# Odd layer of a two-layer backbone: where raw weights land, the order of weight splits and norms, two cells moved between stages, and the first loads of attention

## The chip, the cores and the metric

The kernel runs on one core of one Trainium2 chip. The metric is the device time of one execution in microseconds (us). A core has TensorE (matmuls, PE in the profile; weight loads are PEld), VectorE (DVE), ScalarE (ACT), GpSimd (POOL) and SyncE (SP), each with an instruction queue of its own that is worked off in order. In this kernel SP, POOL and ACT also issue DMA transfers.

## The reference, cut to what matters

Two layers run over 2048 latent tokens and 256 context tokens (16 and 2 tiles of 128). Layer 0 is the even mixer; layer 1, which the change touches, is the odd mixer:

```python
def odd_mixer(h, hc, w_in, q_gain, k_gain, rpb, w_out, update_ctx):
    def heads(u):
        bsz, n, _ = u.shape
        q, k, v, z = jnp.split(u, 4, axis=-1)
        sh = lambda t: t.reshape(bsz, n, C_HEADS, C_HD)
        return rms_norm(sh(q), q_gain), rms_norm(sh(k), k_gain), sh(v), z

    q_x, k_x, v_x, z_x = heads(jnp.dot(h, w_in))
    q_c, k_c, v_c, z_c = heads(jnp.dot(hc, w_in))
    o = neighborhood_attention(q_x, k_x, v_x, k_c, v_c, rpb)
    y = jnp.dot(o.reshape(h.shape[0], h.shape[1], C_WIDTH) * jax.nn.silu(z_x), w_out)
```

`h` and `hc` are the normalised and modulated tokens (1024 wide), `w_in` is 1024 x 4096, there are 16 heads of 64, and the attention of a token sees a window of 8 rows by 16 columns of the token grid, with a bias and a column mask, and the context tokens.

## The kernel before

**Numbers in two parts.** A float32 operand is split into a high part (rounded to the engine's fp32r) and a low part (the rest). A product is three matmuls, high x high, high x low and low x high (`mm3_steps`, L129 to L131 in the profile), accumulated in one bank. A raw weight tile of 128 x 512 is copied by ScalarE to the high part (L106 `w0h<-wraw`) and subtracted by VectorE to the low part (L383 `w0l<-wraw,w0h`).

**Weights of layer 1.** `w_in` is cut into eight blocks j of 512 columns: 0 and 1 are q, 2 and 3 k, 4 and 5 v, 6 and 7 z. Four fit on chip at a time. `OD_PLACE` gives each block one of four places, which the tiles `w0` to `w3` name: blocks 2, 3, 0, 1 take places 0, 1, 2, 3, and later blocks 4, 5, 6, 7 take the same ones. `od_steps` loads a block in eight steps k of 128 rows, through `split_steps` (L366): a raw tile in the ring `wraw` of three buffers, a load on SP (L380), and the two halves of the split. It is a generator that yields after each second step. `pump` takes one such stride after every fourth step of the stage's matmuls, from the first generator in the list `ahead`.

**Cells.** A cell (t, j) is tile t of 128 tokens times block j: 24 matmuls into one bank. `stream` runs cells in a given order and prepares (`prep`, with the normalisation L328, transposes L331, and the two parts of the result L343 and L344) or reloads the next tile where one is done; when a block has had its last cell, `done(j)` appends the generator of the block that follows in its place (`nxt`).

**odd_qk** runs blocks 2, 3, 0, 1 over all tiles. After a q or k cell, ScalarE squares the bank, VectorE sums by head (L1238), GpSimd raises to the power -0.5 (`rpow`, L200 and L202), and VectorE multiplies the bank by it (L1241, `onat`). The cell then waits in `pend`, and `fin` is called for it at the sixth step of a later cell: four transposes on TensorE (L1249), copies by ScalarE and VectorE, and stores to scratch in HBM: Q1 and K1 by SP, K1t by GpSimd (L1286, four of 512 columns at once where four tiles have been collected). The last two tiles, 16 and 17, run block by block at the end: 0, 1, 2, 3 and then 6. Block 6 is half of the gate z: `gate` (tanh on ScalarE, L1301 on VectorE), transposed and stored to z1 by GpSimd (L1253).

**odd_vz** runs the rest, tiles from the last to the first. It begins with (17, 7), (16, 7), (17, 4), (16, 4), (17, 5), (16, 5). A v cell is copied by ScalarE and stored to V1 by GpSimd (`store_v`); a z cell is gated and transposed (L1341). Between them `weave` puts the steps of `maxes`, 0.57 of them for a step of a cell: it finds the largest score of each query and head (matmuls L1376 and L1383, VectorE L1389), with tiles `mk`, `mq`, `mtab`, the memsets of `mz` (L1350) and a mask added by GpSimd (L1361). The results go to M1.

**odd_attention** loads by SP, through `load` (L111): per pair of heads j the queries (`q`, with a row from M1), the context's keys `kc`, four chunks of keys `kt`, values `ov` from V1 and V1c, and the bias tables `tab`, two of 128 x 1034, to which GpSimd adds the column mask `maskk` (L1479). Scores (`st`, L1482 and L1483) of the context's keys need no table; those of the chunks get one added by VectorE (L1646) before ScalarE's exponential. VectorE sums the context's exponentials (L1505), GpSimd the others (L1521). The order of the first loads before is: q(0,1), kt chunk 0, V, tables, kc, q(0,0), kt chunk 1, V1c, maskk.

A program orders the instructions of each engine from a list schedule; `issue_after` puts what is issued within it behind a given instruction.

Of the kernel before, what the change touches and what calls it, by code (L numbers as in the profile page):

```python
# [17 lines left out]
P = 128  # L18
# [70 lines left out]
class Kern:  # L89
    def __init__(self, tc, nc, ins, scr):  # L90
        self.tc, self.nc, self.i, self.scr = tc, nc, ins, scr
        self.n = 0
        self.ahead, self.calls, self.chain = [], 0, None
# [64 lines left out]
    def pump(self):  # L158

        self.calls += 1  # L160
        while self.ahead and self.calls % 4 == 0:
            if next(self.ahead[0], self) is not self:
                break
            self.ahead.pop(0)
# [32 lines left out]
    def rpow(self, out, in_, mul, add):  # L197
# [4 lines left out]
        g.tensor_tensor(out=out, in0=out, in1=self.mhalf[:, : shp[1]], op=ALU.pow)  # L202
# [830 lines left out]
    def even_mix(self, e1, win, hT):  # L1033
# [3 lines left out]
        with ExitStack() as es:  # L1037
# [94 lines left out]

            def ahead():
                for j in (2, 3):
                    yield from self.od_steps(win, j, ws)
# [60 lines left out]
    def od_steps(self, dst, j, ws):  # L1196
        n = self.OD_PLACE[j]
        steps = self.split_steps(dst, j, ws[n // 2], self.i["w_od"][:, j], KD, 512, f"w{n}", 1)
        for k, _ in enumerate(steps):
            if k % 2:  # L1200
                yield

    def odd_qk(self, ws, win, hT):
# [7 lines left out]
        with ExitStack() as es:  # L1211
# [5 lines left out]
            self.ahead += [self.od_steps(win, 0, ws), self.od_steps(win, 1, ws)]  # L1217
            pend, kt = [], {}

            def cell(t, j):  # L1220
# [4 lines left out]
                                       (lambda k: wh[:, k, :], lambda k: wl[:, k, :]), range(KD))  # L1225
# [15 lines left out]
                nc.vector.tensor_tensor(out=n[:].rearrange("p (h d) -> p h d", h=8), in0=ps[:],  # L1241
                                        in1=ss[:].unsqueeze(2).to_broadcast([P, 8, 64]), op=ALU.mult)
                pend.append((t, j, n))

            def fin(t, j, n):
# [9 lines left out]
                self.act(hi[:], ps[:], AF.Copy, scale=qkg[:, z : z + 1])  # L1255
# [3 lines left out]
                if z == 0 or t < NCT:  # L1259
# [7 lines left out]
                    else:  # L1267
                        store_k((hi, lo), j0, t * P, P)
# [10 lines left out]
                if r0 == 6:  # L1279
                    store_k(kt.pop(j), j0, CTX + g * 512, 512)  # L1280

            def store_k(parts, j0, o, w):

                for u, x in enumerate(parts):
                    for i in range(2):
                        nc.gpsimd.dma_start(self.K1t[j0 : j0 + 4, i, u * 64 : u * 64 + 64, o : o + w].rearrange("j d t -> d j t"),  # L1286
                                            x[i * 64 : i * 64 + 64].bitcast(F32))

            nxt = {2: 4, 3: 5, 0: 6, 1: 7}
            done = lambda j: j in nxt and self.ahead.append(self.od_steps(win, nxt[j], ws))  # L1290
            cells = self.cells(list(range(NT)), (2, 3, 0, 1), lambda t, j: j > 1 or t >= NCT)[:-8]
            cells += [(t, j) for j in (0, 1, 2, 3, 6) for t in (NT - 2, NT - 1)]
            for _ in self.stream(cells, hT, cell, lambda t: self.prep(1, t, self.x1, pp, ("px", 2)), done):
                self.pump()
            while pend:
                fin(*pend.pop(0))

# [18 lines left out]
    def odd_vz(self, ws, win, hT):  # L1316
# [3 lines left out]
        with ExitStack() as es:  # L1320
# [6 lines left out]
            def cell(t, j):  # L1327
# [4 lines left out]
                                          (lambda k: wh[:, k, :], lambda k: wl[:, k, :]), range(KD))  # L1332
# [76 lines left out]
            cells = [(t, j) for j in (7, 4, 5) for t in (NT - 1, NT - 2)]  # L1409
# [5 lines left out]
    def odd_attention(self, out, right, left, wout):  # L1415
# [4 lines left out]
        with ExitStack() as es:  # L1420
# [56 lines left out]
            def mask(tabs):  # L1477
                for tb in tabs:
                    nc.gpsimd.tensor_tensor(out=tb[:], in0=tb[:], in1=mk[:], op=ALU.add)  # L1479
# [340 lines left out]
```

## Time and profile before

| | us |
|---|---|
| time, median of 3 runs (lowest to highest) | 3648.87 (3647.48 to 3651.03) |
| the profiled execution: its time | 3651.72 |
| its span on the core | 3649.9 |
| mean granted TensorE clock | 0.985 of full |
| odd_qk, from the first matmul on layer 1's weights | about 2150 to 2602 of the span |
| odd_vz | about 2602 to 3065 |
| odd_attention | about 3065 to 3475 |
| output projection | from about 3475 |

How to read the rows below: in the view of waits a row says which engine and line waited, for which instruction, how long in total, how many times, and the longest. In a row of slices stand the stretch, its length, the busy time of TensorE, weight loads, VectorE, ScalarE and GpSimd with their counts, the granted clock, and what the DMA engines did. A row of the timeline gives start and length in us, the engine, the line, the operation, out<-in, and the idle time ahead of it with what ended it. A row of the chain of waits gives start, length and what was waited for or worked on.

### The profile page before, as it was taken

To read this page: it belongs to the slowest core of one execution; us is meant where nothing else is said; L and a number is where in the kernel's file an instruction comes from. 1 tells how busy PE (TensorE), PEld (TensorE's weight loads), DVE (VectorE), ACT (ScalarE), POOL (GpSimd) and SP (SyncE) were. 2 spreads that over 40 slices of the span, in tenths; PEclk is the share of its full clock that TensorE was granted. 3 is DMA by queue.
4 is the path that set the end of the run, shared out by engine and by line. 5 is a ranking of instruction groups with operands and counts; after the bars stand their busy time and mean duration, and the time that the engine had idled before them with its cause. 6 is when DMAs were issued, how large, how long until landed. Compare 5 with 4: busy or idle time off the path is not lost.

```text
span 3649.9 us, 51809 instructions
## 1 busy us (share of the span) xinstructions
PE 3552.6 (97%) x18404; PEld 2750.0 (75%) x18404; DVE 2355.6 (65%) x4860; ACT 1433.1 (39%) x2741; POOL 1200.8 (33%) x1336
## 2 busy tenths in 40 slices
PE   8999999999999999999999999999899999999899
PEld 6988998888886666665657878888688887555577
DVE  4677666888876666688664435545578784666721
ACT  5545551111115555555553224444422223555510
POOL 1433330101011222112311234333344434777743
PEclk9999999999999999999999999999999999999999
DMA  7455472222242232334533544445743437778554
GB/s 255 146 154 157 135 207 82 86 76 89 74 131 66 76 102 72 93 92 116 164 98 116 186 160 126 146 142 170 226 145 123 140 119 204 209 206 220 176 179 149
DMA packets 364372, 512.19 MB, mean 140 GB/s; under 512 B 25825, under 2 KB 243889, under 8 KB 358210
## 3 DMA queue, kind: packets, MB, share of 16 engines
q1 hardware_dynamic: 322642, 425.49, 39.5%
q0 software_dynamic: 19872, 55.92, 5.2%
q10 hardware_dynamic: 21600, 27.46, 2.1%
q8 instruction: 146, 2.39, 0.3%
q14 instruction: 112, 0.92, 0.1%
HBM read 329.38 MB, written 179.37 MB: 139 GB/s over the span
## 4 chain that ended last, share of the span: by engine, by line
PE 71%; issue 15%; DVE 5%; POOL 4%; DMA 4%; ACT 2%; POOLq 0%; SPq 0%; DVEq 0%; ACTq 0%
PE av L945 7%; PE gm L129 6%; PE gm L131 6%; PE gm L130 6%; PE st L1003 4%; PE st L1004 4%; PE st L1005 4%; PE o L1515 2%; PE st L129 2%; PE st L131 2%; PE st L130 2%; PE st L1482 2%; PE pj L129 2%; PE pj L131 2%; PE pj L130 2%
## 5 line engine op out<-in xcount | busy, mean ns | idle before, releaser
L994 DVE TENSOR_TENSOR acc<-acc,apt 128x512 f32<-128x512 f32 x512 | 368.7, 743 | 163.1 <-ACT apt L106 160.4
L106 ACT ACTIVATE apt<-st 128x512 f32<-128x512 f32 (+1 forms) x592 | 343.1, 593 | 290.8 <-PE st L1005 258.9
L662 DVE TENSOR_REDUCE mm<-mx 128x1 f32<-128x512 f32 (+1 forms) x656 | 393.0, 629 | 91.1 <-PE mx L661 82.8
L945 PE MATMUL av<-apt,av 128*64 128x512 f32 (+1 forms) x1184 | 279.1, 594 | 0.0
L1003 PE MATMUL st<-aq,akh 97*128 97x512 f32 x576 | 249.2, 433 | 4.2 <-ACT apt L106 4.2
L661 PE MATMUL mx<-mk,mq 96*128 96x512 f32 (+1 forms) x656 | 238.6, 372 | 0.0
L1004 PE MATMUL st<-aq,akh 96*128 96x512 f32 x576 | 230.0, 399 | 0.0
L1005 PE MATMUL st<-aq,akl 96*128 96x512 f32 x576 | 229.6, 399 | 0.0
L106 ACT ACTIVATE opt<-opt 128x930 f32<-128x930 f32 (+9 forms) x144 | 119.2, 830 | 247.9 <-POOL opt L1686 139.8
L1389 DVE CUSTOM_DVE_ANT_1 mx<-mx,mtab 128x217 f32<-128x217 f32 (+11 forms) x576 | 184.5, 338 | 49.5 <-PE mx L1383 37.0
L106 ACT ACTIVATE u<-gm 128x352 f32<-128x352 f32 (+1 forms) x144 | 70.3, 495 | 357.9 <-PE gm L131 208.2
L1646 DVE TENSOR_TENSOR opt<-st,tab 128x64 f32<-128x64 f32 (+10 forms) x576 | 142.8, 316 | 87.0 <-PE st L1483 60.7
L945 PEld LDWEIGHTS av<-apt,av 128*64 128x64 f32 x1184 | 80.4, 137 | 153.8 <-issue 152.2
L1521 POOL TENSOR_TENSOR oacc<-oacc,opt 128x682 f32<-128x682 f32 (+9 forms) x144 | 169.8, 1202 | 28.9 <-ACT opt L106 27.7
L1003 PEld LDWEIGHTS st<-aq,akh 97*128 97x128 f32 x576 | 109.3, 190 | 86.9 <-issue 45.0
L661 PEld LDWEIGHTS mx<-mk,mq 96*128 96x128 f32 x656 | 122.8, 188 | 11.7
L1005 PEld LDWEIGHTS st<-aq,akl 96*128 96x128 f32 x576 | 110.4, 192 | 25.4
L1004 PEld LDWEIGHTS st<-aq,akh 96*128 96x128 f32 x576 | 110.7, 192 | 17.5
L106 ACT ACTIVATE x<-px,modB,modA 128x128 f32<-128x128 f32 x272 | 99.1, 468 | 58.2 <-PE px L331 36.0
L1482 PE MATMUL st<-q,kt 128*128 128x480 f32 (+5 forms) x256 | 99.7, 391 | 22.5 <-DVE opt L1646 17.9
L815 POOL TENSOR_TENSOR gsf<-gsf,D 64x512 f32<-64x512 f32 x17 | 24.8, 1459 | 276.8 <-DVE D L792 276.8
L129 PE MATMUL gm<-w1h,hhi 128*128 128x512 f32 x288 | 115.1, 400 | 0.0
(576 smaller groups left out, 10020.6 us busy)
## 6 DMA issues: line engine op xcount, KB each, us to landing
q<-Q SPq DMA_DIRECT2D x48, 512.0 KB
H<-x ACTq DMA_DIRECT2D x36, 512.0 KB
adaw<-ada_w SPq DMA_DIRECT2D x64, 256.0 KB
x<-H SPq DMA_DIRECT2D x32, 512.0 KB
wraw<-w_od SPq DMA_DIRECT2D x64, 256.0 KB
K1t<-okt POOLq DMA_DIRECT2D x32, 512.0 KB, 7.7
kt<-K1t SPq DMA_DIRECT2D x32, 512.0 KB
mtab<-rpb_q SPq DMA_DIRECT2D x16, 899.0 KB
```

Source lines behind the costliest of these rows:

```text
L106: return self.nc.scalar.activation(out, in_, func, **kw)
L129: self.nc.tensor.matmul(out, lh(k), rh(k), start=j == 0, stop=False)
L130: self.nc.tensor.matmul(out, lh(k), rl(k), start=False, stop=False)
L131: yield self.nc.tensor.matmul(out, ll(k), rh(k), start=False, stop=j == n - 1)
L661: mm = nc.tensor.matmul(ps[:, :w], q[:A_QK, (t % 6) * P : (t % 6) * P + P], k[:A_QK, k0 : k0 + w], start=True, stop=True)
L662: nc.vector.tensor_reduce(out=m[:, t, n : n + 1], in_=ps[:, :w], axis=AX.X, op=ALU.max)
L945: nc.tensor.matmul(O[j, nb][i * 64 : i * 64 + 64, :w], V[j, kt // TT][:, kt % TT, i * 64 : i * 64 + 64], pts[i][:, :w], start=n == 0, stop ...
L994: self.add = nc.vector.tensor_tensor(out=acc[i][:, :w], in0=a[:, :w], in1=pts[i][:, :w], op=ALU.add)
L1003: nc.tensor.matmul(ps[:, :w], kh[: A_QK + 1, i, kq], qh[: A_QK + 1, :w], start=True, stop=False)
L1004: nc.tensor.matmul(ps[:, :w], kh[:A_QK, i, kq], ql[:A_QK, :w], start=False, stop=False)
L1005: mm = nc.tensor.matmul(ps[:, :w], kl[:A_QK, i, kq], qh[:A_QK, :w], start=False, stop=True)
L1389: nc.vector.tensor_tensor_reduce(out=s, in0=s, in1=tb[:, ri : ri + rn, ci : ci + cn], scale=1.0, scalar=-3e38, op0=ALU.add, op1=ALU.max, a ...
```

## The change

- Raw weights of layer 1 land in the low part's own places: the low part is eight tiles of [128, 512] in place of one of [128, 8, 512], and the raw rows k of a block are loaded into the tile that will hold its low part k + 1 (only k = 7 goes to the ring `wraw`). The split of k is written over the raw tile of k - 1, which has been split by then. A load waits until the tile in that place has been read for the last time. One generator goes through a list `todo` of blocks, with up to four loads ahead of the splits, two loads and two splits per stride.
- Splits are issued behind marks on the same engines: the latest Square, tanh or scaled copy on ScalarE, the latest norm multiply on VectorE.
- The four K1t stores of 512 columns go out one per four steps of a cell, each behind the latest power on GpSimd, in place of all at once. `pend` is also emptied one further in a cell of block 4.
- (16, 4) and (17, 4) are run at the end of odd_qk, behind block 6, in place of near the start of odd_vz.
- Attention's first loads come in the order q(0,1), kc, q(0,0), tables, mask, kt chunk 0, V, kt chunk 1, V1c, and the mask again; the first mask is loaded into the place of a query tile that is not yet in use.

```diff
         while self.ahead and self.calls % 4 == 0:
-            if next(self.ahead[0], self) is not self:
+            with ExitStack() as es:
+                for x in self.marks.values():
+                    es.enter_context(self.tc.issue_after(x.ins))
+                r = next(self.ahead[0], self)
+            if r is not self:
                 break
             self.ahead.pop(0)
 
...
-        g.tensor_tensor(out=out, in0=out, in1=self.mhalf[:, : shp[1]], op=ALU.pow)
+        self.power = g.tensor_tensor(out=out, in0=out, in1=self.mhalf[:, : shp[1]], op=ALU.pow)
...
+            self.todo = [2, 3]
+
             def ahead():
-                for j in (2, 3):
-                    yield from self.od_steps(win, j, ws)
+                yield from self.od_steps(win, ws)
                 for t in range(2):
                     hT[t] = self.prep(1, t, self.x1, pp, ("pj", 4))
...
-    def od_steps(self, dst, j, ws):
-        n = self.OD_PLACE[j]
-        steps = self.split_steps(dst, j, ws[n // 2], self.i["w_od"][:, j], KD, 512, f"w{n}", 1)
-        for k, _ in enumerate(steps):
-            if k % 2:
-                yield
+    def od_steps(self, dst, ws):
+
+        nc, todo, raw, k = self.nc, self.todo, [], KD
+
+        def split(w, parts, pool, n, k):
+            hi, lo = parts
+            lo.append(self.tl(pool, [P, 512], f"w{n}l{k}", F32R, bufs=1))
+            self.act(hi[:, k, :], w[:])
+            nc.vector.tensor_tensor(out=lo[k][:], in0=w[:], in1=hi[:, k, :], op=ALU.subtract)
+
+        while raw or todo or k < KD:
+            for i in range(2):
+                if raw and (len(raw) >= 4 or k == KD and not todo):
+                    split(*raw.pop(0))
+                if k == KD and todo:
+                    j, k = todo.pop(0), 0
+                    n = self.OD_PLACE[j]
+                    pool = ws[n // 2]
+                    dst[j] = self.tl(pool, [P, KD, 512], f"w{n}h", F32R, bufs=1), []
+                if k < KD:
+                    w = self.tl(pool, [P, 512], f"w{n}l{k + 1}", bufs=1) if k < KD - 1 else self.tl(self.prp, [P, 512], "wraw", bufs=3)
+                    nc.sync.dma_start(w[:], self.i["w_od"][:, j, k])
+                    raw.append((w, dst[j], pool, n, k))
+                    k += 1
+            yield
+
+    def od_ahead(self, dst, ws, *js):
+
+        self.todo += js
+        if not self.ahead:
+            self.ahead.append(self.od_steps(dst, ws))
...
-            self.ahead += [self.od_steps(win, 0, ws), self.od_steps(win, 1, ws)]
-            pend, kt = [], {}
+            self.od_ahead(win, ws, 0, 1)
+            pend, kt, out_k = [], {}, []
...
                 for n, _ in enumerate(steps):
-                    if n == 5 and pend and (len(pend) > 1 or j == 6):
+                    if n == 5 and pend and (len(pend) > 1 or j in (4, 6)):
                         fin(*pend.pop(0))
+                    if n % 4 == 1 and out_k:
+                        with self.tc.issue_after(self.power.ins):
+                            out_k.pop(0)()
                     yield
+                if j == 4:
+                    n = self.tl(sp, [P, 512], "onat", bufs=4)
+                    self.act(n[:], ps[:].rearrange("p h d -> p (h d)"))
+                    self.store_v(t, 0, n)
+                    return
                 if j == 6:
                     n = self.tl(sp, [P, 512], "onat", bufs=4)
                     self.gate(n, ps[:].rearrange("p h d -> p (h d)"))
+                    self.marks["a"] = self.last_tanh
...
-                self.act(sq[:], ps[:].rearrange("p h d -> p (h d)"), AF.Square)
+                self.marks["a"] = self.act(sq[:], ps[:].rearrange("p h d -> p (h d)"), AF.Square)
...
-                nc.vector.tensor_tensor(out=n[:].rearrange("p (h d) -> p h d", h=8), in0=ps[:],
-                                        in1=ss[:].unsqueeze(2).to_broadcast([P, 8, 64]), op=ALU.mult)
+                self.marks["d"] = nc.vector.tensor_tensor(out=n[:].rearrange("p (h d) -> p h d", h=8), in0=ps[:],
+                                                        in1=ss[:].unsqueeze(2).to_broadcast([P, 8, 64]), op=ALU.mult)
...
-                    store_k(kt.pop(j), j0, CTX + g * 512, 512)
+                    out_k.extend(store_k(kt.pop(j), j0, CTX + g * 512, 512))
 
             def store_k(parts, j0, o, w):
 
-                for u, x in enumerate(parts):
-                    for i in range(2):
-                        nc.gpsimd.dma_start(self.K1t[j0 : j0 + 4, i, u * 64 : u * 64 + 64, o : o + w].rearrange("j d t -> d j t"),
-                                            x[i * 64 : i * 64 + 64].bitcast(F32))
+                def store(u, x, i):
+
+                    nc.gpsimd.dma_start(self.K1t[j0 : j0 + 4, i, u * 64 : u * 64 + 64, o : o + w].rearrange("j d t -> d j t"),
+                                        x[i * 64 : i * 64 + 64].bitcast(F32))
+
+                return [lambda u=u, x=x, i=i: store(u, x, i) for u, x in enumerate(parts) for i in range(2)]
 
             nxt = {2: 4, 3: 5, 0: 6, 1: 7}
-            done = lambda j: j in nxt and self.ahead.append(self.od_steps(win, nxt[j], ws))
+            done = lambda j: j in nxt and self.od_ahead(win, ws, nxt[j])
             cells = self.cells(list(range(NT)), (2, 3, 0, 1), lambda t, j: j > 1 or t >= NCT)[:-8]
-            cells += [(t, j) for j in (0, 1, 2, 3, 6) for t in (NT - 2, NT - 1)]
+            cells += [(t, j) for j in (0, 1, 2, 3, 6, 4) for t in (NT - 2, NT - 1)]
             for _ in self.stream(cells, hT, cell, lambda t: self.prep(1, t, self.x1, pp, ("px", 2)), done):
                 self.pump()
             while pend:
                 fin(*pend.pop(0))
+            for f in out_k:
+                f()
+            self.marks = {}
...
-            cells = [(t, j) for j in (7, 4, 5) for t in (NT - 1, NT - 2)]
+            cells = [(t, j) for j in (7, 5) for t in (NT - 1, NT - 2)]
...
-            def mask(tabs):
+            def mask(tabs, mk):
                 for tb in tabs:
-                    nc.gpsimd.tensor_tensor(out=tb[:], in0=tb[:], in1=mk[:], op=ALU.add)
+                    nc.gpsimd.tensor_tensor(out=tb[:], in0=tb[:], in1=mk, op=ALU.add)
+
+            def load_mask(mk):
+                self.load(mk, self.i["maskk"].rearrange("p (r c) -> p r c", r=NR))
+                return mk
...
             Q[0, 1] = query(0, 1)
+            kc[0] = keys(0, 0, CTX, kcp, "kc")
+            Q[0, 0] = query(0, 0)
+            tabs[0] = tables(0)
+            first = self.tl(qa, [P, SEQ], "q10", bufs=2)[:, : NR * NC]
+            mask(tabs[0], load_mask(first.rearrange("p (r c) -> p r c", r=NR)))
             kt.append(chunk(0, 0))
             V[0] = values(0)
-            tabs[0] = tables(0)
-            kc[0] = keys(0, 0, CTX, kcp, "kc")
-            Q[0, 0] = query(0, 0)
             kt.append(chunk(0, 1))
             values_ctx(0, V[0])
-            mk = self.tl(ap, [P, NR, NC], "maskk", bufs=1)
-            self.load(mk[:], self.i["maskk"].rearrange("p (r c) -> p r c", r=NR))
-            mask(tabs[0])
+            mk = load_mask(self.tl(ap, [P, NR, NC], "maskk", bufs=1)[:])
```

Each use of a low part `wl[:, k, :]` becomes `wl[k][:]`.

More of the change, by code (lines that the diff above doesn't have):

```diff
@@ L92, in __init__ @@
         self.n = 0
-        self.ahead, self.calls, self.chain = [], 0, None
+        self.ahead, self.calls, self.chain, self.marks = [], 0, None, {}
     def pool(self, es, name, bufs=1, space=None, **kw):
@@ L1254, in fin @@
                     return
-                self.act(hi[:], ps[:], AF.Copy, scale=qkg[:, z : z + 1])
+                self.marks["a"] = self.act(hi[:], ps[:], AF.Copy, scale=qkg[:, z : z + 1])
                 j0 = (j % 2) * 4
@@ L1267, in fin @@
                     else:
-                        store_k((hi, lo), j0, t * P, P)
+                        for f in store_k((hi, lo), j0, t * P, P):
+                            f()
                     return
@@ L1296, in odd_qk @@
                 fin(*pend.pop(0))
+            for f in out_k:
+                f()
+            self.marks = {}
     def gate(self, out, in_):
@@ L1331, in cell @@
                 yield from self.mm3_steps(ps[:], (lambda k: hi[:, k, :], lambda k: lo[:, k, :]),
-                                          (lambda k: wh[:, k, :], lambda k: wl[:, k, :]), range(KD))
+                                          (lambda k: wh[:, k, :], lambda k: wl[k][:]), range(KD))
                 n = self.tl(sp, [P, 512], "ovz", bufs=3)
@@ L1618, in odd_attention @@
                             with self.tc.issue_after(self.psum.ins):
-                                mask(tabs[j + 1])
+                                mask(tabs[j + 1], mk)
                     elif s % 2 and s < 16:
```

2 lines of the change are left out of this document (1 added, 1 removed).

## The prediction

> **What bounds the kernel now.** I read the page first, then the waits of TensorE, then slices of 25 us, and only where a slice fell short of 25 us the timelines and the chain of waits.
>
> ```profile
> span 3649.9 us, 51809 instructions
> PE 3552.6 (97%) x18404; PEld 2750.0 (75%) x18404; DVE 2355.6 (65%) x4860; ACT 1433.1 (39%) x2741; POOL 1200.8 (33%) x1336
> ```
>
> TensorE is the bound: 3552.6 of 3649.9 us. The change removes no matmul and adds none, so it can only return time in which TensorE waits or runs slowly. The waits in and around `odd_qk`:
>
> ```profile
> PE tp L1249 <- DVE onat L1241: 7.4, 2, 6.2
> PE tp L1249 <- ACT oqh L106: 3.6, 1, 3.6
> PE tp L1341 <- DVE ovz L1301: 2.8, 1, 2.8
> PE px L331 <- DVE x L328: 2.8, 1, 2.8
> ```
>
> And by slices (length, busy PE, PEld, DVE, ACT, POOL, granted clock, DMA share, GB/s):
>
> ```profile
> 2150.00:2175.00 25.00, 23.08 (x105) 18.63 (x103) 14.51 (x22) 12.70 (x23) 11.65 (x13) 1.00 0.59 189
> 2175.00:2200.00 25.00, 23.99 (x112) 19.63 (x113) 13.93 (x24) 12.14 (x29) 14.10 (x20) 0.93 0.67 195
> 2525.00:2550.00 25.00, 23.13 (x105) 18.84 (x104) 11.74 (x20) 9.57 (x20) 7.06 (x9) 0.93 0.35 113
> 2550.00:2575.00 25.00, 25.00 (x121) 20.65 (x120) 16.80 (x27) 13.99 (x24) 8.30 (x8) 1.00 0.82 235
> 2575.00:2600.00 25.00, 15.28 (x67) 11.59 (x65) 14.16 (x24) 14.48 (x25) 6.25 (x8) 0.84 0.82 249
> 2600.00:2625.00 25.00, 20.76 (x89) 16.96 (x90) 6.33 (x14) 6.54 (x12) 9.09 (x8) 0.88 0.91 304
> ```
>
> The row of 2550 is the steady state, which the slices between 2200 and 2525 share: no idle time and full clock. The stage loses time in three places: its start (idle 1.92 + 1.01 = 2.9 us, and 0.07 x 25 = 1.75 us by the clock), one spot at 2525 (1.87 us and 0.07 of the clock), and its end with the start of `odd_vz` (9.72 + 4.24 = 13.96 us, and by the clock while busy 0.16 x 15.28 + 0.12 x 20.76 = 4.9 us: 18.9 us). Whatever the change does to weights, norms and stores is worth at most the first and the third: 4.7 + 18.9 = 23.6 us. The spot at 2525 is the last tile's own norm and transposes, whose order the change leaves; it stays.
>
> **Part 1, the start of the stage.**
>
> ```profile
> 2169.34 4.44 DMA wraw<-w_od
> 2175.07 0.76 DVE x L328
> 2175.88 1.97 PE px L331 x8
> L129 PE MATMUL gm<-w3h,hhi x256: 387/391/775, 2197.5 to 3041.3; 128*128 128x512 f32 x128
> ```
>
> These are the chain of waits and, in the last row, the first and last start of the matmuls that read `w3h`. The normalisation of the next tile, x L328 (0.75 us), stands on VectorE behind a weight split, which waits for a raw load of 4.44 us through the ring of three buffers. In the changed order x comes ahead of all eight splits of `w3l`, behind those of `w2l` only; and the raw tiles land four ahead instead of in a ring. The first matmul on `w3h` comes at 2197.5, some 20 us later, so the splits that fall behind x are not late. I take away 4.5 of the 4.7 us; bounds 0 (the splits of `w2l` are late in the same way) and 4.7.
>
> **Part 2, the end of the stage.**
>
> ```profile
> 2585.91 6.88 DMA wraw<-w_od
> 2593.47 0.69 DVE L383 TENSOR_TENSOR w1l<-wraw,w1h 128x512 fp32r<-128x512 f32 x1 [3.73 <-ACT w1h L106]
> 2594.60 0.68 DVE L1241 TENSOR_TENSOR onat<-gm,oss 128x512 f32<-128x512 f32 x1
> 2588.57 1.66 POOL L202 TENSOR_TENSOR oss<-oss,mhalf 128x8 f32<-128x8 f32 x1
> ```
>
> The norm's multiply (L1241) could have started when its power was done, at 2590.23, but stood behind a split whose raw tile landed at 2592.79 (6.88 us in the chain of waits): 4.4 us late. The power was itself behind K1t stores on GpSimd. Now the splits are placed behind the latest norm and its Square, and the K1t stores go one per four steps behind the latest power. The two onat waits (7.4) and the oqh wait (3.6) are of this kind: 11.0 us. A norm's own path is the power's 1.66 us, the multiply's 0.68 and two instructions (a Square, a sum) that I put at the multiply's size: about 4 us, an estimate. One more cell of 24 matmuls covers it. I take all 11.0; bounds 6 and 11.0.
>
> The start of `odd_vz` (2.8 us) hangs on another queue:
>
> ```profile
> 2602.80 2.48 POOL L1286 DMA_DIRECT2D K1t<-okt  x4 [0.33 <-ACT okt L106]
> 2605.27 0.76 POOL L1253 DMA_DIRECT2D z<-oqh  x1
> 2605.27 10.53 DMA z<-oqh
> 2616.12 1.02 DVE L1350 MEMSET mz<- 64x512 f32 x2 [6.96 <-ACT ovz L106]
> 2618.58 0.23 PE gm L129
> ```
>
> The memsets of `mz` take the place of the stored tile, so VectorE stands until the z1 store has landed (10.53 us), and the gates behind them let TensorE wait at L1341. In the change the two cells (16,4) and (17,4) come after those of z1; the last z1 store is issued at the sixth step of the last cell, some 4.3 us before the stage ends instead of about 1 us after it. It would land near 6 us into `odd_vz`, and TensorE has 48 matmuls of 0.23 us (the last row, a step of the chain on TensorE; 11 us in all, and 5.5 us for a cell of 24) before it needs the gate. The V1 stores of the new last cells follow it on the same queue, and later tiles take their place too. I take 2.0 of 2.8; bounds -3 (the V1 stores land as late as z1 did) and 2.8.
>
> The clock goes with the waits: 4.9 x 13.0/13.96 = 4.6 us, of which I take 3.5, since 1.87 us of idle time were enough at 2525 for 0.93. The Trainium skill (TensorE: Matmul & The Clock Gate, "What's actually happening") has the gate pass half or all pulses, judged over windows of some 3.4 us. By it a dip costs an estimated 1.7 us, the three dips 5.1 us rather than my 6.6, and the forecast would stand 1.5 us higher; the rows fit both.
>
> Moving the two cells adds a due date: weight 4 is needed at the eleventh cell of the tail.
>
> ```profile
> 2547.32 0.94 SPq L380 DMA_DIRECT2D wraw<-w_od  x2
> 2583.45 0.69 DVE L383 TENSOR_TENSOR w0l<-wraw,w0h 128x512 fp32r<-128x512 f32 x1 [0.81 <-ACT w0h L106]
> ```
>
> In the trace w0 to w3 name the four places; here w0 holds weight 4, w1 weight 5, w2 weight 6 and w3 weight 7. Weight 4's last split ended at 2584.1, 36.8 us after the first of 24 loads (12.3 us per weight). Eight cells from 2547.3 without stalls end at 2547.3 + 8 x 5.5 = 2591.3. So at the old pace it is 7.2 us early, and the pace may go to 44/3 = 14.7 us per weight before it is late. But each load now waits for the last read of the tile in whose place it lands, and the splits wait for norms. I put 3 us against this and smaller waits; bounds 0 and 10.
>
> Part 2 together: 11.0 + 2.0 + 3.5 - 3 = 13.5 us gained.
>
> **Part 3, attention's first loads.**
>
> ```profile
> PE st L1482 <- DVE opt L1646: 3.3, 3, 1.9
> 3050.00:3075.00 25.00, 22.00 (x98) 17.77 (x97) 7.19 (x18) 6.49 (x13) 6.37 (x5) 0.97 0.90 232
> 3036.68 1.07 SPq L111 DMA_DIRECT2D kt<-K1t  x2
> 3037.98 0.41 SPq L111 DMA_DIRECT2D ov<-V  x1
> 3064.83 0.34 SPq L111 DMA_DIRECT2D maskk<-maskk  x1
> kt<-K1t SPq DMA_DIRECT2D x2, 512.0 KB
> ov<-V SPq DMA_DIRECT2D x1, 1024.0 KB
> 3068.60 0.29 PE L1482 MATMUL st<-q,kt 128*128 128x288 f32 x1
> 3068.98 4.71 POOL L1479 TENSOR_TENSOR tab<-tab,maskk 128x1034 f32<-128x1034 f32 x2 [2.48 <-PE st L1482]
> 3066.68 3.58 DVE L1505 TENSOR_REDUCE wo<-opt 128x512 f32<-128x1024 f32 x3 [21.81 <-ACT opt L106]
> 3071.39 0.65 DVE L1646 TENSOR_TENSOR opt<-st,tab 128x32 f32<-128x32 f32 x4 [1.13 <-POOL tab L1479]
> 3071.96 1.23 DVE L1505 TENSOR_REDUCE wo<-opt 128x512 f32<-128x1024 f32 x1
> L1389 DVE CUSTOM_DVE_ANT_1 mx<-mx,mtab x44: 200/296/651, 2999.8 to 3028.6; 128x217 f32<-128x217 f32 x6, 128x155 f32<-128x155 f32 x4, 128x105 f32<-128x105 f32 x4, 128x465 f32<-128x465 f32 x4
> ```
>
> The mask is issued last, so the tables are ready at 3071.4 and the first adds follow. With the mask ahead of kt and V the tables are ready earlier, but four sums stand on VectorE ahead of the first add: 3066.68 + 4 x 1.23 = 3071.6, as late as now. What goes is the sum in between (1.23 us at 3071.96) and, with the other order of the first scores, part of the 1.9. Idle there is 3.0 us in the slice of 3050, and with the clock after it some 5.5 us: bounds -6 and 5.5. I take 1.5.
>
> The lower bound: the kc loads wait for the last maxima (the last starts at 3028.6), which the two cells taken out of `odd_vz` push some 10.9 us closer to attention, to about 3039.5 on this scale; all later loads stand behind them in SP's queue. kt and V go out about 13 us later than at 3036.68, and at a DMA share of 0.90 and 232 GB/s their 2 MB take 9 us: about 3059 to 3066. kt is read at 3068.6. It is in time with little to spare; the second tables and the copy of maskk do not matter here.
>
> **Part 4, the rest.** `odd_vz` is two cells shorter with the same maxima, so VectorE is fuller there. The nearest row for a gate that comes late in it is the 2.8 us wait at L1341. I put 1 us against it; bounds -4 and 1.
>
> **Sum.** 4.5 + 13.5 + 1.5 - 1 = 18.5 us. The profiled execution took 3651.72 us around its span of 3649.9, so 3633.2; it lies 2.85 us above the median of the runs, 3648.87, so I forecast 3630 for a median.
>
> **Rivals.**
> A. The transfers bound the end of the stage. From 2550 to 2625 they moved 25 x (235 + 249 + 304) = 19.7 MB; at the best slice, 304 GB/s, that is 65 us, so 75 us can shrink by 10 and not by 13.5. Against it: some of these bytes are first loads of `odd_vz` that are not due. Result 4.5 + 10 + 1.5 - 1 = 15: 3634. The Trainium skill (DMA: Bandwidth & Descriptors, "Issuing engines are not separate DMA queues") says that all issuers share the same 16 engines; the high shares beside these rates agree.
> B. The waits only move. Start regained, but tail at its lower bounds (6 - 3 + 1.5 - 3 = 1.5) and attention late by 4: 4.5 + 1.5 - 4 - 1 = 1 us, 3648. For it: in-order queues keep a stall alive if one link is left.
> C. Slower: landing in the low part ties each load to TensorE, and weight 4 isn't there. If only two loads were in flight, each at the 6.88 us of the longest in this tail, a weight would take some 4 x 6.88 = 27.5 us, three 82.5 against 44 us of cover: 38.5 us late in place of the 3 us of the sum: 3630 - 3 + 38.5 = 3666. It decides from 14.7 us per weight on, and the kernel is slower by over 7.3 us from some 24 us on (3 x (24.4 - 14.7) = 29). Against it: loads go four ahead.
> D. Everything at its upper bound: 4.7 + 18.9 + 5.5 = 29 us, 3620.
>
> **How the numbers follow.** The forecast with its own range 3624 to 3638 has 0.46, A 0.16, B 0.16, C 0.12, D 0.10. A measurement of this kernel can tell some 0.2%, 7.3 us, from no change. Faster by more takes the forecast, A, D and a little of B: 0.74. Within it: most of B, 0.13. Slower: C and a late start of attention, 0.13. The range runs from D's 3620 across B to 3654, and leaves out the lowest end and most of C.
>
> **What would show it.** Right: no wait of px for x at the start and a slice there at 1.00; the onat and oqh waits gone from the last 50 us of `odd_qk`; no more than 1 us at the first `ovz` transposes; slices of `odd_vz`'s first 25 us full. Wrong: waits of gm for `w0h` or `w0l` at the first (t,4) cell (C); the same idle time with another releaser (B); first scores waiting for kt or V loads (part 3). If the spot at 2525 vanishes, my claim that its order is untouched is wrong.

## The result, and the profile after

| | kernel before | changed kernel |
|---|---|---|
| median of 14 runs (lowest to highest) | 3652.11 us (3646.30 to 3658.15) | 3643.20 us (3636.56 to 3645.65) |
| span of the profiled execution | 3649.9 us | 3638.5 us |
| ratio to before | | 0.9973 (95%: 0.9965 to 0.9981) |

The kernel got faster by 0.27%: 8.9 us between the medians, 9.9 us by the ratio. I had said 18.5 us of 3649, 0.5%: the direction was right, the size was about twice what came.

The page of the changed kernel, its first two rows:

```profile
span 3638.5 us, 51802 instructions
PE 3544.1 (97%) x18404; PEld 2745.5 (75%) x18404; DVE 2361.8 (65%) x4860; ACT 1431.9 (39%) x2741; POOL 1201.7 (33%) x1336
```

The waits of TensorE from 2140 us to 3110 us, the rows of over 1 us, and the slices that answer to those shown of before. Line numbers have moved: L347 here is L343 before, L1288 is L1249, L1346 is L1301, L1386 is L1341, L1428 is L1383, L1531 is L1482. hhi and hlo are the high and the low part of a tile's normalised tokens.

```profile
PE gm L129 <- DVE hhi L347: 4.2, 2, 2.3
PE st L1531 <- DMA kt<-K1t: 2.9, 1, 2.9
PE mx L1428 <- DVE mm L1423: 2.7, 2, 2.4
PE tp L1386 <- DVE ovz L1346: 1.7, 1, 1.7
PE st L1531 <- DVE opt L1695: 1.3, 3, 0.8
PE mx L1428 <- DVE mm L1434: 1.2, 1, 1.2
PE mx L1421 <- ACT mz L106: 1.2, 1, 1.2
```

```profile
2150.00:2175.00 25.00, 24.18 (x116) 19.66 (x114) 13.29 (x21) 12.57 (x24) 13.16 (x18) 1.00 0.71 229
2175.00:2200.00 25.00, 23.03 (x100) 18.48 (x101) 14.72 (x26) 12.18 (x27) 12.77 (x18) 0.93 0.59 178
...
2525.00:2550.00 25.00, 23.13 (x111) 19.00 (x111) 11.31 (x19) 8.98 (x19) 8.05 (x10) 1.00 0.67 211
2550.00:2575.00 25.00, 25.00 (x121) 20.63 (x120) 18.62 (x30) 15.91 (x30) 8.52 (x8) 1.00 0.81 251
2575.00:2600.00 25.00, 25.00 (x119) 20.61 (x118) 15.86 (x26) 16.54 (x29) 10.89 (x16) 1.00 0.82 221
2600.00:2625.00 25.00, 23.82 (x113) 19.51 (x112) 6.41 (x11) 4.86 (x8) 9.73 (x4) 1.00 0.78 270
...
2675.00:2700.00 25.00, 22.61 (x105) 18.50 (x104) 19.97 (x64) 5.91 (x11) 10.37 (x8) 0.93 0.31 102
```

The slice of 2575 is full (15.28 before), and the waits for onat and oqh are gone. The start of the stage is as it was: idle 0.82 + 1.97 = 2.8 us and a clock of 0.93, against 2.9 and 0.93; the main wait changed its name, from px behind x (2.8 us) to gm behind hhi (2.3 us; the other 1.9 us of that row are the spot at 2525). In odd_vz waits for maxima (mx) stand that were not there before, and at attention's start a wait for a load has taken the place of one for a table.

Totals of single executions cannot carry this further. The stretch ahead of layer 1, the same instructions in each kernel, lost between 421 and 429 us in the profiles below. So I read each stage by itself, by its **loss**: for each matmul the distance from its start to the next one's start, less the usual distance for its shape (the 30th percentile in the profile of before), summed over the stage. It holds idle time and slow clock together.

```
loss in us           start  2525  last cells  first 42 us  rest of  first 45 us   rest of
                     of qk  spot  of odd_qk   of odd_vz    odd_vz   of attention  attention
before                5.1   3.9     15.0         3.3          7.8      24.4        203.9
changed               5.3   2.2      0.1         3.1         13.6      26.2        201.5
changed, again        5.2   2.2      0.1         2.9          9.8      25.9        203.7
e1 ring               6.9   3.9      7.4         3.3          9.9      26.0        200.9
e2 no marks           3.9   2.3      0.1         1.7         11.5      25.9        201.0
e3 no move            5.0   3.8      8.4         2.4          7.7      22.8        198.9
e4 old loads          5.0   4.0      0.1         3.0         13.6      33.8        203.5
e5 M1 by ScalarE      5.1   2.2      0.1         3.0          5.3      27.1        201.9
e6 before + e5        6.8   2.3     15.6         2.9          5.5      25.0        199.5
e7 modulate mark      1.8   2.3      0.1         3.4         11.4      28.2        204.1
f1 e5 + e7            1.8   3.8      0.1         3.4          5.7      26.2        194.9
f2 f1 + ratio 0.59    1.8   2.3      0.1         5.5          6.5      22.9        198.7
f3 landing only       4.4   2.3      6.1        10.8          9.4      23.7        197.4
f4 stores at once     4.8   2.2      0.1         2.7         13.2      26.2        203.6
```

The last cells, the tail below, are those from 410 us after the stage's start; odd_vz starts 11.4 us ahead of its first transpose (e4's 33.8 holds 8.0 us that stand just ahead of the first scores of attention's chunks). Between before and the changed kernel the columns give +0.2 - 1.7 - 14.9 - 0.2 + 5.8 + 1.8 - 2.4 = -11.4 us, the difference of the spans. The spot at 2525 is either near 2.2 or near 3.9, with the wait of 1.9 us in both cases; the rest is the clock after it, so the -1.7 there is not a gain of the change. The same chance stands in the other columns: the start of odd_qk is the same program in before and e6, and lost 5.1 and 6.8; the changed kernel lost 13.6 and 9.8 in the rest of odd_vz. So from one profile each a difference under 2 us is not to be read, in "rest of odd_vz" none under 4, and in "rest of attention" none under 5. The first column of attention holds cells in another order; with other groupings of shapes its difference between before and the changed kernel comes out anywhere from 1.8 to 4.5 us. Its sign is firm: the eight profiles with the cells moved, the new order and the maxima at 0.57 lost 25.9 to 28.2 there, before and e6 24.4 and 25.0.

### The profile page after: what moved, and what is told of

It is laid out like the page before. It is cut to its first block, busy times and chain, and to the rows that moved or that the text cites. A ratio compares the mean times of both kernels' runs of the same rounds, so it can differ in the third digit from the quotient of the medians.

```text
span 3638.5 us, 51802 instructions
## 1 busy us (share of the span) xinstructions
PE 3544.1 (97%) x18404; PEld 2745.5 (75%) x18404; DVE 2361.8 (65%) x4860; ACT 1431.9 (39%) x2741; POOL 1201.7 (33%) x1336
## 5 line engine op out<-in xcount | busy, mean ns | idle before, releaser
L1434 DVE CUSTOM_DVE_ANT_1 mx<-mx,mtab 128x465 f32<-128x465 f32 (+14 forms) x576 | 184.2, 338 | 50.5 <-PE mx L1428 35.3
L1570 POOL TENSOR_TENSOR oacc<-oacc,opt 128x682 f32<-128x682 f32 (+10 forms) x144 | 169.3, 1198 | 20.9 <-ACT opt L106 19.7
L1531 PE MATMUL st<-q,kt 128*128 128x480 f32 (+5 forms) x256 | 98.8, 389 | 27.5 <-DVE opt L1695 20.0
L129 PE MATMUL gm<-w0h,hhi 128*128 128x512 f32 x288 | 116.2, 404 | 2.3 <-DVE hhi L347 2.3
```

Source lines behind the costliest of these rows:

```text
L129: self.nc.tensor.matmul(out, lh(k), rh(k), start=j == 0, stop=False)
L1434: nc.vector.tensor_tensor_reduce(out=s, in0=s, in1=tb[:, ri : ri + rn, ci : ci + cn], scale=1.0, scalar=-3e38, op0=ALU.add, op1=ALU.max, a ...
```

## The experiments

My theories after the result. Theory 1: the loss in odd_vz comes from a subtract of VectorE that GpSimd holds up. Theory 2: the start of odd_qk is held by weight splits ahead of the modulate on ScalarE (the eight activations x<-px,modB,modA that scale and shift a tile's transposes). The rivals: the shorter odd_vz is too full for VectorE, and the third tile's chain is too long for its cover.

**The changed kernel again** (no edit).

> The changed kernel once more. If its losses are set by the order of instructions, the profile shows them at the same places: a gm wait for hhi of some 2.3 us about 2175 us, a wait of 2.4 us in TensorE near 2686 us and one of 1.7 us near 2891 us, each behind a subtract of VectorE (hlo, L361) of over 5 us, and slices of 2550 to 2600 full. If they come from chance, they move or go. Time 0.997 of before, 0.996 to 0.998.

The ratio to before, as are all ratios below, is 0.9972 (0.9962 to 0.9982). The losses stand at the same places, with hlo subtracts of 5.07 us at 2684.0 and 5.96 us at 2885.5. Their places are set by the order of instructions; their size varies (9.8 us and 13.6 us in the rest of odd_vz).

**e5, the M1 stores issued by ScalarE.**

```diff
-                            nc.gpsimd.dma_start(self.M1[h, ...
+                            nc.scalar.dma_start(self.M1[h, ...
```

> Changed kernel; only the stores of M1 (four small DMAs per head) are issued by ScalarE and not by GpSimd. Theory 1 (VectorE's subtract hlo<-x,hhi, both operands in SBUF, cannot get in while GpSimd issues these DMAs and then stands through the mask add behind them): no hlo of L361 over 2.5 us, the waits of TensorE near 2686 and 2891 go, and with them their slow clock: 6 to 9 us less than the changed kernel, ratio to before about 0.995. Rival 1 (odd_vz is two cells shorter, so VectorE is too full and late whatever GpSimd does): the waits stay or move within the stage, less than 2 us gained.

In the changed kernel, the timelines of VectorE, GpSimd and TensorE near 2686 us:

```profile
2682.86 5.71 DVE L361 TENSOR_TENSOR hlo<-x,hhi 128x1024 fp32r<-128x1024 f32 x1
```

```profile
2681.35 2.38 POOL L1449 DMA_DIRECT2D M<-mr  x4
2683.74 3.73 POOL L1407 TENSOR_TENSOR mtab<-mtab,maskq 128x1798 f32<-128x1798 f32 x1
```

```profile
2689.22 0.68 PE L1428 MATMUL mx<-mk,mz 128*128 128x480 f32 x1 [2.40 <-DVE mm L1423]
```

The subtract starts while GpSimd issues the stores, and ends at 2688.57, 1.1 us after the end of the mask add behind them: it got in only when both were over. It takes 1.22 us by itself. The next maximum (L1423) waits behind it, and TensorE for that. In before this happened once (6.25 us at 2787.7), in the changed kernel twice. The same place with the stores on ScalarE:

```profile
2681.05 3.20 POOL L1406 TENSOR_TENSOR mtab<-mtab,maskq 128x1798 f32<-128x1798 f32 x1 [8.48 <-DMA mtab<-rpb_q]
2684.33 3.73 POOL L1407 TENSOR_TENSOR mtab<-mtab,maskq 128x1798 f32<-128x1798 f32 x1
```

```profile
2686.14 3.01 DVE L361 TENSOR_TENSOR hlo<-x,hhi 128x1024 fp32r<-128x1024 f32 x1
```

```profile
2675.00:2700.00 25.00, 25.00 (x126) 21.03 (x126) 21.12 (x86) 7.10 (x12) 8.12 (x5) 1.00 0.43 151
2875.00:2900.00 25.00, 25.00 (x126) 21.05 (x125) 20.58 (x83) 7.22 (x12) 8.55 (x6) 1.00 0.43 150
```

With no issue between them the second add runs right behind the first and is half done when the subtract comes. The subtract still waits for its end (3.01 us, over the 2.5 that I had allowed), but TensorE no longer waits for what follows: both slices are full at full clock. The rest of odd_vz loses 5.3 us against 9.8 and 13.6. Over all runs with the two cells moved, it is 5.3 to 6.5 us in the three with the stores on ScalarE (e5, f1, f2) and 9.8 to 13.6 in the seven with them on GpSimd. The total did not show it: ratio 0.9977 (0.9968 to 0.9986), where I had expected 0.995. Theory 1 holds for the stage; the rival, that VectorE is simply too full, falls, since VectorE is no less busy in the slice of 2675 (21.12 us) than in the changed kernel (19.97).

**e6, the same edit in the kernel before.**

> Kernel before; only the stores of M1 are issued by ScalarE. Theory 1: its one wait in odd_vz behind a long hlo (6.25 us at 2787.7, wait 2.0 us at 2792) goes: 2 to 4 us less than before, ratio 0.999, and the two kernels then differ by the end of odd_qk alone. Rival 1: nothing over 1 us.

The rest of odd_vz fell from 7.8 to 5.5 us, its wait behind the long subtract went; the subtract took 3.47 us. Ratio 1.0006 (0.9996 to 1.0015): 2.3 us can't be seen in the total, whose interval leaves out the expected 0.999.

**e7, the modulate as a mark.**

```diff
-                self.act(h[:, k, :], ps[g][:, k % 4, :], AF.Identity, ...
+                last = self.act(h[:, k, :], ps[g][:, k % 4, :], AF.Identity, ...
...
-        nc.scalar.dma_start(self.H[l, t], x[:])
+        nc.scalar.dma_start(self.H[l, t], x[:]); self.marks.update({"a": last} if l else {})
```

> Changed kernel; the last modulate activation of a tile's preparation becomes a mark too, so that weight splits issued after it stand behind it on ScalarE. Theory 2 (at the start of odd_qk the third tile's modulate stands behind two pairs of splits on ScalarE, 1.15 us each): hhi is ready 1 to 2 us earlier, the gm wait of 2.3 us falls to under 1 us, 1.5 to 4 us gained with the clock. Rival 2 (the tile's own chain from its sum of squares to hhi is longer than the one cell that covers it): the wait stays at 1.5 us or more, and under 1 us is gained.

The changed kernel's ScalarE and VectorE at the start of odd_qk:

```profile
2171.92 1.14 ACT L106 ACTIVATE w3h<-w3l 128x512 fp32r<-128x512 f32 x2
2172.96 0.58 ACT L106 ACTIVATE osq<-gm 128x512 f32<-128x512 f32 x1
2173.44 1.15 ACT L106 ACTIVATE w3h<-w3l 128x512 fp32r<-128x512 f32 x2
2174.48 2.90 ACT L106 ACTIVATE x<-px,modB,modA 128x128 f32<-128x128 f32 x8
```

```profile
2170.22 0.75 DVE L332 TENSOR_SCALAR x<-x,ssx 128x1024 f32<-128x1024 f32 x1 [1.03 <-POOL ssx L206]
2176.02 0.43 DVE L347 CAST hhi<-x 128x512 fp32r<-128x512 f32 x1
```

x comes at 2170.22, 4.9 us earlier than before and ahead of every split of `w3l`, as I had said. But its transposes (from 2172.53) meet two pairs of splits on ScalarE, and hhi comes at 2176.02. With the mark one pair is left in front, and TensorE's row is

```profile
2176.81 0.50 PE L129 MATMUL gm<-w0h,hhi 128*128 128x512 f32 x1 [1.28 <-DVE hhi L347]
```

against a wait of 2.32 us in the changed kernel; the granted clock of that slice is 1.00 and not 0.93, and the start loses 1.8 us and not 5.2. The runs with this edit all lose 1.8 us there (e7, f1, f2), the others 3.9 to 6.9. Ratio 0.9964 (0.9952 to 0.9977), which overlaps with that of the changed kernel. The wait kept more than the 1 us of theory 2, so a part of the chain is the tile's own; the gain of 3.4 us is in the range of theory 2, and over half of it is the clock.

**e1, the ring again.**

```diff
-                if raw and (len(raw) >= 4 or k == KD and not todo):
+                if raw and (len(raw) >= 2 or k == KD and not todo):
...
-                    w = self.tl(pool, [P, 512], f"w{n}l{k + 1}", bufs=1) if k < KD - 1 else self.tl(self.prp, [P, 512], "wraw", bufs=3)
+                    w = self.tl(self.prp, [P, 512], "wraw", bufs=3)
```

> Changed kernel, but raw weights land in the ring of three buffers again, split two behind the load; marks, dealt stores, moved cells and attention's order stay. If the landing place is what removed the tail's loss (15.0 us over the steady pitch before, 0.1 after), most of it comes back: 8 us or more. If the order of splits behind norms did it, the tail loses under 4 us more, perhaps with a wait for the weights of the first (t,4) cell.

The tail lost 7.4 us, with these waits:

```profile
PE tp L1288 <- DVE okt L1317: 2.7, 1, 2.7
PE gm L129 <- ACT onat L106: 2.7, 1, 2.7
```

That is 7.3 us more than the changed kernel, between my two cases (8 or more, under 4). The ratio is 1.0002 (0.9992 to 1.0011): with the ring, the rest of the change is worth nothing that the total shows. The ring of three holds fewer loads ahead of the splits (two in place of four), so this edit takes back the place and the depth together; a deeper ring, which would tell them apart, was not tried. "Landing place" stands for both below.

**e2, no marks; f4, K1t stores at once.** In e2 `pump` takes its stride without `issue_after`; in f4 `store_k` is run through on the spot.

> Changed kernel without the marks: splits are not ordered behind Square, copies or norms; loads still land in the low parts, stores are still dealt. If the order did it, the onat and oqh waits return: tail loss 6 us or more. If the deeper loads alone did it (data there in time, so that a split in front costs 0.7 us only), the tail loses under 3 us.

> Changed kernel with the four K1t stores of 512 columns issued at once. If dealing them behind the power matters, a norm's power stands 2.5 us behind them on GpSimd and an onat wait of 1 to 3 us returns in the tail. If the cells cover it, the tail stays at its steady pitch and the total at 0.997.

The tail loses 0.1 us in both, as in the changed kernel; ratios 0.9970 (0.9959 to 0.9981) and 0.9978 (0.9968 to 0.9989). With the two cells moved, neither the order of the splits nor the dealt stores is needed for the tail once the raw tiles are there in time; each was taken out with the other still in place. A split whose data has come takes 0.68 us ahead of a norm's multiply (in e2 at 2555.26, the multiply at 2555.86), where before the multiply was 4.4 us late.

**e3, (16,4) and (17,4) back in odd_vz.**

```diff
-            cells += [(t, j) for j in (0, 1, 2, 3, 6, 4) for t in (NT - 2, NT - 1)]
+            cells += [(t, j) for j in (0, 1, 2, 3, 6) for t in (NT - 2, NT - 1)]
...
-            cells = [(t, j) for j in (7, 5) for t in (NT - 1, NT - 2)]
+            cells = [(t, j) for j in (7, 4, 5) for t in (NT - 1, NT - 2)]
```

> Changed kernel with (16,4) and (17,4) back in odd_vz. By my prediction the wait of ovz at its start returns (2 to 4 us with the clock), since the last z1 store lands late again; the tail's other 11 us stay away. Rival: the start of odd_vz loses the same 3 us as in both kernels, in one form or the other, and the move was worth nothing there, or the two long subtracts in odd_vz fall elsewhere.

Its waits from 2560 to 2640 us:

```profile
PE tp L1288 <- ACT oqh L106: 5.7, 1, 5.7
PE tp L1386 <- DVE ovz L1346: 2.0, 1, 2.0
PE tp L1288 <- DVE okt L1317: 0.7, 1, 0.7
```

The tail loses 8.4 us; without the two cells the last `fin` steps have no matmuls of the stage left to hide behind. The wait for a gate (ovz) at the start of odd_vz is back, as expected, but that start loses no more than in the changed kernel (2.4 us against 3.1). And odd_vz has one subtract of over 5 us (6.2 us) in place of two and loses 7.7, attention's first 45 us lose 22.8, and the ratio is 0.9972 (0.9962 to 0.9981), that of the changed kernel. The move takes 8.3 us from the tail and gives most or all of them back: 2 to 6 in odd_vz, where the second long subtract stands, and 3 at attention's start.

**e4, attention's first loads as before.**

> Changed kernel with attention's first loads in the order of before. The first 45 us of attention lost 24.4 us over the steady pitch before and 26 after. If the new order costs (kt's second chunk lands late, 2 to 3 us of DMA waits), the loss is 24 to 25 with the opt waits of 3 us back: 1 to 2 us less than the changed kernel. If the loss comes from the later end of the maxima, it stays at 26 or grows.

```profile
PE st L1531 <- DMA q<-Q: 7.9, 1, 7.9
```

A miss: neither of my numbers. The first scores wait 7.9 us for q(0,0); ratio 0.9984 (0.9974 to 0.9995). With the two cells moved, that order no longer works: SP's queue stood 16.5 us for z stores ahead of these loads. The new order costs 1.8 us there over before, and saves 7.6 over this.

**f3, the landing place alone.** Marks, dealt stores, the move and the order of loads undone.

> Only the landing place is changed (no marks, stores of K1t at once, (16,4) and (17,4) in odd_vz, attention's loads in the order of before). If the landing alone removed the waits behind late splits, the tail loses some 8 us over the steady pitch, as without the move, against 15.0 before: ratio 0.997 to 0.998. If it needs the dealt stores or the marks, the tail loses 11 us or more.

The tail lost 6.1 us of 15.0, but the start of odd_vz 10.8, waiting 6.7 us for a gate behind the z1 store, which took 13.26 us to land; ratio 0.9982 (0.9971 to 0.9992). In e3, with marks, dealt stores and the new order of loads, that start lost 2.4. So the marks or the dealt stores are worth some 8 us there while the cells stay in odd_vz; once the cells are moved, taking out either one costs nothing there (e2 1.7, f4 2.7). Which of the two it is was not tried.

**f1, both edits; f2, with the maxima woven in at 0.59.**

> Changed kernel with both: the modulate of a tile's preparation is a mark, and ScalarE issues the M1 stores. If the two losses are independent, the start of odd_qk loses under 2 us over the steady pitch and the middle of odd_vz under 6 (5.2 and 9.8 to 13.6 in the changed kernel): some 8 us less than the changed kernel, ratio to before 0.995. If one only hands its gain on (a wait for kt or V1c at attention's start grows by as much), the ratio stays at 0.997.

> As f1_mod_m1, and the maxima are woven in at 0.59 and not 0.57 per step, so that they end some two cells earlier and SP's first loads of attention go out earlier. If attention's first 45 us lose 27 us because these loads are late, they fall to 23 to 25: 2 to 4 us less than f1_mod_m1. If VectorE in odd_vz has no room for it, waits of gates and maxima grow there by as much or more.

f1: ratio 0.9955 (0.9941 to 0.9970), span 3633.3 us; the gains of the two stages add, start 1.8 and rest of odd_vz 5.7. f2: 0.9959 (0.9945 to 0.9972); attention's first 45 us fell to 22.9 and its waits for kt went, so the loads were late because the maxima ended late, but odd_vz lost 2.9 us more. f1 is the fastest kernel here by its ratio; its interval and that of the changed kernel overlap by a little, and f1 and f2 can't be told apart.

## Why the prediction was off, step by step

The terms of the sum, against the loss of before less that of the changed kernel and of its second profile (the spot at 2525 and the rest of attention are left out):

| term | forecast, us gained | changed | changed, again |
|---|---|---|---|
| part 1, start of odd_qk | 4.5 | -0.2 | -0.1 |
| part 2, end of odd_qk and start of odd_vz | 13.5 | 15.1 | 15.3 |
| part 3, start of attention | 1.5 | -1.8 | -1.5 |
| part 4, rest of odd_vz | -1 | -5.8 | -2.0 |
| sum | 18.5 | 7.3 | 11.7 |

The sum failed at the start, which gained nothing, and in the two stages behind the moved cells, where more was lost than I had put against them.

**Part 1, the start: wrong, 4.5 us forecast and none measured.** The failed step is "In the changed order x comes ahead of all eight splits of `w3l`", taken as enough. It was true on VectorE. I had not followed the same tile through ScalarE, where splits stood ahead of its modulate; the wait went from px to hhi (loss 5.1 us before, 5.2 and 5.3 after). e7 gave 3.4 us of it. It is what I had named as the sign of rival B, the same idle time with another releaser.

The forecast's reading of the clock holds up better. In the changed kernel's dip at the start the matmuls from 2178.4 to 2180.5 us start 0.43 us apart, where 0.23 is usual; from 2177.07 to 2180.85 nine steps take 3.78 us in place of 2.07, so the dip cost 1.7 us, the price of the prediction's other estimate and the difference of 3.9 and 2.2 at the spot of 2525. But that price would not have moved the forecast by 1.5 us: the 6.6 us are all that the clock took in the rows (1.75 + 4.9), and the sum took only some 5.1 of them (1.6 and 3.5).

**Part 2, the end of odd_qk: near in size, partly by luck, and wrong in cause.** I took 11.0 us of waits and 3.5 of clock, less 3 for new waits; 14.9 went, and no new wait came: no matmul waits for the weights of block 4. The 3 us that were not needed made up for the 2.0 us at the start of odd_vz that did not come. I put it down to "the splits are placed behind the latest norm" and the dealt stores. e2 and f4 show that, with the cells moved, neither is needed. It is the landing place (15.0 to 6.1 in f3) and the two cells at the end (8.4 without them in e3, 0.1 with them). At the start of odd_vz I took 2.0 us; the wait for the gate went, as argued from the z1 store's time, but the first maxima wait for their tables and queries instead, and the loss stayed at 3 us.

**Part 3, attention's loads: wrong sign, within the bounds.** 1.5 us of gain forecast, 1.5 to 1.8 lost. Without the move the new order may gain a little, 0.9 to 1.6 (e3's 22.8 against f3's 23.7 and 24.4 of before, which have the same order and differ by 0.7 themselves). "It is in time with little to spare" was the step: TensorE waited 2.9 us for kt, because all loads behind kc wait in SP's queue.

```profile
3030.88 1.14 SPq L111 DMA_DIRECT2D kc<-K1t  x2
3041.00 6.57 SPq L111 DMA_DIRECT2D q<-Q  x3
...
3048.96 0.43 SPq L111 DMA_DIRECT2D q<-maskk  x1
3049.43 1.09 SPq L111 DMA_DIRECT2D kt<-K1t  x2
```

```profile
SPq L111 <- DMA z<-ozt: 14.0, 2, 9.0
```

```profile
3058.52 4.70 POOL L1524 TENSOR_TENSOR tab<-tab,q 128x1034 f32<-128x1034 f32 x2 [3.06 <-DMA q<-maskk]
```

These are SP's issues, its wait and GpSimd's mask in the changed kernel. Attention starts at 3053.8 here; q(0,0) stood 9 us behind kc, until a z store of odd_vz had landed, and the mask did not land before 3058.5. kc went out 23 us ahead of attention, close to the 25 that I had reckoned (3039.5 against 3065), but kt only 4.4 us ahead, where I had some 15. I had counted the wait of kc, not the next one.

**Part 4, the rest of odd_vz: mis-sized.** 1 us forecast, 2.0 and 5.8 measured in two profiles. I priced it by a late gate; it was the subtract held by GpSimd (e5, f1 and f2 lose no more there than before), a thing that the profile of before showed once, at 2787.7, and that I did not look into.

Of the **rivals**, A fell: the slices of 2550 to 2600 are full at 251 and 221 GB/s. C fell: weight 4 was in time. B was half right, and at other places than it named: the tail's waits did not move, those of the other three places did. D, all terms at their upper bounds, fell with parts 1 and 3.

**What to carry to other kernels.** Follow a tile that is late through every engine of its chain, not only the one whose queue the trace names; a wait removed at one link shows up at the next. Before ordering work behind other work, ask if its data is late: with the data there in time, the order of the splits was worth nothing in this tail. Moving work out of a stage shortens the cover of everything that was paced by that stage's end, so price the stage after it as well.

## What the runs showed of the hardware

A subtract of VectorE with both operands in SBUF took 1.22 us by itself and 5.1 to 6.3 us where it met GpSimd's DMA issue with an add behind it; it did not get in between the two. It did get in between two adds that stood back to back, when it began during the first. In e1, GpSimd and VectorE:

```profile
2632.58 3.20 POOL L1406 TENSOR_TENSOR mtab<-mtab,maskq 128x1798 f32<-128x1798 f32 x1
2635.74 4.69 POOL L1407 TENSOR_TENSOR mtab<-mtab,maskq 128x1798 f32<-128x1798 f32 x1
```

```profile
2633.56 3.31 DVE L361 TENSOR_TENSOR hlo<-x,hhi 128x1024 fp32r<-128x1024 f32 x1
```

The subtract ends 1.09 us after the first add, and the second takes 4.69 us in place of 3.73. So it is a start during the issue of the stores that costs VectorE the add as well. Why the turn falls to GpSimd there, no run shows.

GpSimd can be the one that waits, too. In the changed kernel, GpSimd and VectorE:

```profile
2654.78 4.59 POOL L1407 TENSOR_TENSOR mtab<-mtab,maskq 128x1798 f32<-128x1798 f32 x1
```

```profile
2654.55 1.24 DVE L361 TENSOR_TENSOR hlo<-x,hhi 128x1024 fp32r<-128x1024 f32 x1
```

Here the subtract was first, and the add took 4.59 us, 0.86 over its 3.73. The Trainium skill (SBUF — State Buffer, "Who interferes with whom") says that a VectorE instruction with two SBUF inputs contends with a GpSimd instruction that reads SBUF, and that the one issued first blocks the other entirely. The trace agrees: 1.24 beside 4.59 with the subtract first, and 3.01 beside 3.73 in e5, where the add was first. The 5.71 beside 3.73 goes beyond it: that subtract began 0.88 us before the add and still stood through it.

A short wait can cost more than itself: 2.32 us at the start came with a granted clock of 0.93 in its slice, 1.28 us with 1.00. It does not always: the same 1.9 us at 2525 came with 0.93 in the profile of before and with 1.00 in that of the changed kernel. In the two slices of the start the idle time fell by 1.5 us (0.82 + 1.97 against 0 + 1.28) and the loss by 3.4.
